# Hybrid Mamba-2 and latent-attention trunk on one core: probabilities of whole off-diagonal chunks split with queries on partitions and turned by DMA

## The chip, the cores and the metric

The kernel runs on one core of one Trainium2 chip. A core has a matrix engine (TensorE, PE in the profile), a vector engine (VectorE, DVE), a scalar engine (ScalarE, ACT), a general engine (GpSimd, POOL) and a queue engine that mostly issues transfers (SyncE, SP). They run side by side, each takes its instructions in order, and they wait for each other through semaphores. Sixteen DMA engines move data for all. The metric is the device time of one execution in microseconds; the median of several executions is given.

## The reference: what is computed

Two layers over 2048 tokens of width 1024: a Mamba-2 layer (in-projection, causal convolution, chunked state-space scan, gated out-projection), then a latent-attention layer with 16 heads whose keys and values come once from a compressed latent; a final RMS norm. The change lies in the attention:

```python
for i in range(S // Q_BLOCK):
    q0 = i * Q_BLOCK
    kv_len = q0 + Q_BLOCK
    s = einsum('bqhd,bkhd->bhqk', q_nope[:, q0:kv_len], k_nope[:, :kv_len]) + \
        einsum('bqhr,bkr->bhqk', q_rope[:, q0:kv_len], k_rope[:, :kv_len])
    s = s.astype(float32) * scale
    mask = (q0 + local)[:, None] >= arange(kv_len)[None, :]
    p = softmax(where(mask, s, -inf), axis=-1)
    outs.append(einsum('bhqk,bkhd->bqhd', p, v[:, :kv_len]))
```

A query sees the keys up to its own place, so the work of a block of queries grows with its place in the sequence. Queries and keys have 96 numbers a head (64 and 32 rotary), values 64.

## The kernel before, in words

The program has three stages: the Mamba layer with the projections of the attention (`layers`, L212), the attention itself (`attention`, L855, and `heads`, L863), and the gated output projection with the final norm (`back`, L999). Tiles are placed and semaphores set by a tile framework, which also chooses the order of each engine's instructions; in the attention PE's order alone is that of the program text (L860).

All products are made of parts: a float32 number is split into a high part and a remainder, and three products stand for one (`mm3`, L83). Score products use this; probabilities and values are split into two float16 halves (`pair16`, L114), with the value halves side by side, so that two products do.

`heads` goes over 64 jobs: 16 heads, and in each four blocks of 512 queries (`qb` 0 to 3). It has two streams. The first, `scores` (L879), takes the 128 queries of `j` = 0 to 3 in turn; I call this a row. Its keys, `512*qb + 128*(j+1)`, are cut by `cuts` (L868) into chunks of up to 512, one PSUM bank each: one bank for `qb` 0, up to four for `qb` 3. For each chunk PE makes three products (L85 to L87), a mask is added at the row's last chunk (L903, L905), and DVE takes the maximum over the keys (L906). After the last chunk DVE reduces the maxima to the bias (L910). The exponentials (L918, ACT) write the probabilities `Pr` to SBUF and their sums aside; they are kept in the list `late` and issued one by one with the score products that follow, and the row's sums are added by DVE (L922). The score banks have the tag "mm" with four buffers, so PE cannot start a chunk before the exponential of the chunk four before it has read its bank.

The second stream is the value products. A unit is a block of 128 keys for 512 queries. `turn` (L928) transposes the four 128 x 128 probability blocks on PE (L933) into a bank "tr", and `pair16` splits that bank: ACT writes the high half (L116), DVE the remainder (L117), both scaled by `PSCALE`. `values` (L939) multiplies both halves with the values (L943, L944) into a bank that collects the job's output; the last unit calls `finish` (L948), where ACT copies the bank (L950), SP stores one half (L952) and POOL adds the other in an accumulating store (L956).

PE alternates between the streams by a table written by hand: `CREDIT[qb][j][n]` (L43) says after each score chunk which turns ("T") and value products ("V") follow. They start 20 chunks late (`LAG`), and two turned units are held ahead (`DEPTH`). Loads of the next head's queries, keys and values are issued on POOL (L833 to L847), the output projection's weights on SP (L852). `back` splits those weights by ACT and POOL (L1016, L1017) into tiles "W", which have buffers of their own beside the attention's, and "K", which take over key buffers.

## Time and profile before

| | |
|---|---|
| median of 3 runs | 3239.51 us (3238.54 to 3240.34) |
| the profiled execution | 3238.15 us |
| its span, first to last instruction | 3236.3 us |
| mean granted clock of TensorE | 0.995 |
| busy: PE, DVE, ACT, POOL | 98%, 80%, 64%, 20% of the span |

How to read the rows: a row of the groups names line, engine, operation, tile written and read, shape and count, then the busy time of the group, the mean duration of one in ns, and the idle time before them with what ended it. A row of the waits says which engine and line waited for which, in total, how often and how long at most. Matmuls are pipelined: a row's duration is longer than the step from one start to the next, so PE's cost of one is read from starts in the timeline. The small operations of DVE overlap a little in the same way, so sums of durations come out above the busy time.

### The profile page before, as it was taken

Reading aid. Unit: us, or ns where it says so; the run is one execution under the profiler, and the core shown is the slowest. Engines: PE = TensorE matmul, PEld = TensorE weight load, DVE = VectorE, ACT = ScalarE, POOL = GpSimd, SP = SyncE. Lnnn points to the kernel's source line nnn. Section 1 sums busy time; section 2 is a strip of 40 time slices with the busy share of each in tenths; the row PEclk is TensorE's granted clock in tenths of the full one; section 3 lists DMA queues with packets and bytes.
Section 4 is the critical chain, followed back from the end, with each engine's and each line's share of the span. In section 5 each row is a group of like instructions: output and inputs, shape, how many; then the busy total and the mean of one; then the engine's idle time right before and its main releaser. Section 6 shows DMA issues by size and latency. Waiting matters only on the chain.

```text
span 3236.3 us, 50476 instructions
## 1 busy us (share of the span) xinstructions
PE 3156.2 (98%) x16708; PEld 2563.4 (79%) x16708; DVE 2593.4 (80%) x5490; ACT 2055.2 (64%) x5117; POOL 646.2 (20%) x842
## 2 busy tenths in 40 slices
PE   8999999999999999998999999999999999999998
PEld 6788888888888888887888888777777777777787
DVE  6988888889889888887776765668888888888675
ACT  5666666666657655666555554567777877778522
POOL 1221122221212222222211211222212212223100
PEclk9999999999999999999999999999999999999999
DMA  5333343333433334333466666753443434344385
GB/s 174 108 104 92 118 131 119 105 96 122 140 96 109 90 125 145 104 94 111 132 221 212 236 204 208 246 137 79 82 89 77 97 77 88 77 90 116 81 272 172
DMA packets 210572, 418.91 MB, mean 129 GB/s; under 512 B 27107, under 2 KB 68835, under 8 KB 208869
## 3 DMA queue, kind: packets, MB, share of 16 engines
q1 hardware_dynamic: 168900, 291.39, 28.9%
q0 software_dynamic: 41408, 124.29, 15.7%
q8 instruction: 132, 2.16, 0.3%
q14 instruction: 132, 1.07, 0.1%
HBM read 321.33 MB, written 94.24 MB: 128 GB/s over the span
## 4 chain that ended last, share of the span: by engine, by line
PE 44%; ACT 3%; DMA 2%; DVE 2%; issue 1%; SPq 0%; POOL 0%; ACTq 0%; DVEq 0%
PE mm L85 7%; PE mm L87 7%; PE mm L86 7%; PE tr L933 6%; PE tr L943 3%; PE tr L944 3%; PE tr L86 3%; PE tr L87 3%; PE tr L85 3%; ACT Pr L918 1%; DVE PTs L117 1%; ACT PTs L116 1%; DMA wraw<-in_kv_w_up_dram 1%; PE mm L905 1%; DMA wraw<-in_kv_w_down_dram 0%
## 5 line engine op out<-in xcount | busy, mean ns | idle before, releaser
L117 DVE SCALAR_TENSOR_TENSOR PTs<-tr,PTs 128x512 f16<-128x512 f32 (+3 forms) x640 | 374.7, 607 | 92.6 <-ACT PTs L116 86.0
L116 ACT ACTIVATE PTs<-tr 128x512 f16<-128x512 f32 (+3 forms) x640 | 328.2, 541 | 140.9 <-PE tr L933 140.0
L906 DVE TENSOR_REDUCE mx<-mm 128x1 f32<-128x512 f32 (+2 forms) x631 | 375.5, 607 | 45.4 <-PE mm L87 42.8
L918 ACT ACTIVATE Pr<-mm,nm 128x512 f32<-128x512 f32 (+2 forms) x631 | 395.1, 635 | 23.1 <-DVE nm L910 21.5
L108 ACT ACTIVATE wsp<-wraw 128x512 fp32r<-128x512 f32 (+1 forms) x452 | 251.1, 574 | 171.7 <-PE mm L87 82.4
L109 DVE TENSOR_TENSOR wsp<-wraw,wsp 128x512 fp32r<-128x512 f32 (+1 forms) x452 | 301.8, 680 | 69.7 <-ACT wsp L108 68.9
L85 PE MATMUL mm<-xT,wsp 128*128 128x512 f32 x800 | 321.0, 401 | 0.0
L933 PE MATMUL tr<-pack,Pr 128*128 128x128 f32 x2176 | 317.5, 273 | 0.9 <-ACT Os L950 0.8
L87 PE MATMUL mm<-xT,wsp 128*128 128x512 f32 x800 | 314.1, 393 | 0.0
L86 PE MATMUL mm<-xT,wsp 128*128 128x512 f32 x800 | 312.9, 391 | 0.0
L85 PE MATMUL mm<-K,xT 96*128 96x512 f32 (+2 forms) x639 | 286.7, 449 | 23.1 <-ACT Pr L918 21.7
L933 PEld LDWEIGHTS tr<-pack,Pr 128*128 128x128 f32 x2176 | 253.4, 141 | 49.3 <-ACT Os L950 1.6
L85 PE MATMUL mm<-wsp,xT 128*128 128x512 f32 (+1 forms) x640 | 242.1, 378 | 0.0
L86 PE MATMUL mm<-wsp,xT 128*128 128x512 f32 (+1 forms) x640 | 237.7, 371 | 0.0
L87 PE MATMUL mm<-wsp,xT 128*128 128x512 f32 (+1 forms) x640 | 237.5, 372 | 0.0
L87 PE MATMUL mm<-K,xT 96*128 96x512 f32 (+2 forms) x639 | 231.4, 362 | 0.0
L358 DVE SCALAR_TENSOR_TENSOR cacc<-craw,pack,cacc 128x512 f32<-128x512 f32 x288 | 216.5, 774 | 18.3 <-ACT cacc L356 17.8
L86 PE MATMUL mm<-K,xT 96*128 96x512 f32 (+2 forms) x639 | 231.1, 362 | 0.0
L496 POOL TENSOR_TENSOR Xp<-Xw,Xp 128x512 fp32r<-128x512 f32 x64 | 83.1, 1298 | 697.5 <-ACT Xp L495 393.1
L943 PE MATMUL tr<-PTs,xT 128*128 128x512 f16 (+3 forms) x640 | 222.0, 348 | 0.1
L538 ACT ACTIVATE Xw<-tr,d_wend 128x64 f32<-128x64 f32 x512 | 182.8, 358 | 58.7 <-DVE Xd L534 58.6
L944 PE MATMUL tr<-PTs,xT 128*128 128x512 f16 (+3 forms) x640 | 219.4, 347 | 0.0
(368 smaller groups left out, 8145.9 us busy)
## 6 DMA issues: line engine op xcount, KB each, us to landing
wraw<-in_ssm_w_in_dram SPq DMA_DIRECT2D x256, 256.0 KB, 2.8
big<-cumT SPq DMA_DIRECT2D x64, 512.0 KB, 4.0
wraw<-in_ssm_w_out_dram SPq DMA_DIRECT2D x128, 256.0 KB, 2.6
wraw<-in_ssm_w_in_dram SPq DMA_DIRECT2D x129, 128.0 KB, 2.2
xT<-qn_d POOLq DMA_DIRECT2D x64, 256.0 KB, 4.4
K<-kn_d POOLq DMA_DIRECT2D x15, 1024.0 KB, 9.2
wraw<-in_mla_w_uq_dram SPq DMA_DIRECT2D x36, 256.0 KB, 4.0
hx<-in_x_dram SPq DMA_DIRECT2D x16, 512.0 KB, 4.2
```

The costliest lines, as they stand in the source:

```text
L85: mm(out, l_hi, r_hi, start=start, stop=False)
L86: mm(out, l_hi, r_lo, start=False, stop=False)
L87: mm(out, l_lo, r_hi, start=False, stop=stop)
L108: nc.scalar.activation(hi, src, AF.Copy)
L109: nc.vector.tensor_tensor(lo, src, hi.bitcast(F32), ALU.subtract)
L116: self.nc.scalar.activation(hi, src, AF.Copy, scale=scale)
L117: self.nc.vector.scalar_tensor_tensor(lo, src, scale, hi, ALU.mult, ALU.subtract)
L906: v.tensor_reduce(mx[:, n:n + 1], s[:, :w], AX.X, ALU.max)
L918: nc.scalar.activation(x[:, :w], s[:, :w], AF.Exp, bias=nm, accum_out=sm[:, n:n + 1])
L933: nc.tensor.transpose(pt[:, j * P:(j + 1) * P], st["P"][j][kb], self.ident)
L943: nc.tensor.matmul(st["O"][:, c], vals[h][:, kb, :], u[:, 0], start=kb == 0, stop=False)
L944: nc.tensor.matmul(st["O"][:, c], vals[h][:, kb, :], u[:, 1], start=False, stop=kb == nk - 1)
```

## The change

Probabilities of chunks that lie wholly left of the diagonal block can be turned in another way. `BYDMA = (0, 1, 1, 2)` says for how many leading chunks of a row, by `qb`, this is done: none in `qb` 0, one in `qb` 1 and 2, two in `qb` 3. There, after the exponential, DVE casts the 128 x 512 probabilities to float16 with the queries still on the partitions, POOL subtracts to get the remainder, and SP issues a transposing DMA of the 128 x 1024 pair into a tile `PX`, from which the value products read directly. The scale moves into the exponential's bias (`PSHIFT`, the logarithm of 32768), since halves are now taken before the turn.

The bias is built up: maxima are taken negated, and from a row's second chunk on a small DVE operation keeps the running minimum with the shift added. `cuts` keeps a first chunk of 512 whole (a row of 640 keys is cut 512 + 256 rather than 384 + 256, the mask covering the surplus).

The table is replaced by a rule. Within a job DMA-turned and PE-turned units are mixed by `order`. A job's units may be issued only `GAP` = 5 chunks after its last score chunk. Each score chunk then allows an amount of turning and value work, in estimated microseconds (`T_US`, `V_US`), in proportion to its width; 85% of it is held back until the row's last chunk. The tiles "W" of the last stage move to a pool that is opened after the attention's is closed.

```diff
-CREDIT = (
...
-)
+GAP = 5
+BYDMA = (0, 1, 1, 2)
+T_US, V_US, S_US = 0.436, 0.432, 0.7
-PSCALE = 32768.0
+PSHIFT = 10.397207708399179
...
-    def pair16(self, hi, lo, src, scale=1.0):
-        self.nc.scalar.activation(hi, src, AF.Copy, scale=scale)
-        self.nc.vector.scalar_tensor_tensor(lo, src, scale, hi, ALU.mult, ALU.subtract)
+    def pair16(self, hi, lo, src):
+        self.nc.scalar.activation(hi, src, AF.Copy)
+        self.nc.vector.tensor_tensor(lo, src, hi, ALU.subtract)
...
-                if kv - at == TB + P:
+                if kv - at == TB + P and at:
...
-                    v.tensor_reduce(mx[:, n:n + 1], s[:, :w], AX.X, ALU.max)
+                    m = mx[:, n:n + 1]
+                    v.tensor_reduce(m, s[:, :w], AX.X, ALU.max, negate=True)
                     banks.append((s, w))
-                    yield CREDIT[qb][j][n]
-                nm = self.t(sp, "nm", [P, 1], bufs=4)
-                v.tensor_reduce(nm, mx[:, :nb], AX.X, ALU.max, negate=True)
+                    if n != 0 or nb == 1:
+                        nm, old = self.t(sp, "nm", [P, 1], bufs=6), nm
+                    if nb == 1:
+                        v.tensor_scalar(nm, m, PSHIFT, None, ALU.add)
+                    elif n == 1:
+                        v.scalar_tensor_tensor(nm, m, mx[:, 0:1], shift, ALU.min, ALU.add)
+                    elif n > 1:
+                        v.scalar_tensor_tensor(nm, m, shift, old, ALU.add, ALU.min)
+                    yield qb, w, n == nb - 1
...
                     nc.scalar.activation(x[:, :w], s[:, :w], AF.Exp, bias=nm, accum_out=sm[:, n:n + 1])
+                    if n < BYDMA[qb]:
+                        u = self.t(sp, "Ph", [P, 2, TB], F16, bufs=4)
+                        v.tensor_copy(u[:, 0], x)
+                        nc.gpsimd.tensor_tensor(u[:, 1], x, u[:, 0], ALU.subtract)
+                        if j == 0:
+                            st["X"].append(self.t(sp, "PX", [P, 2, 4, TB], F16, bufs=5))
+                        d = st["X"][n].rearrange("p s k q -> p (s k) q")[:, :, j * P:(j + 1) * P]
+                        nc.sync.dma_start_transpose(d, u.rearrange("p s k -> p (s k)"))
...
+        def order(qb):
+            d, p = list(range(4 * BYDMA[qb])), list(range(4 * BYDMA[qb], 4 * qb + 4))
+            return sorted(d + p, key=lambda kb: kb / len(d) if kb in d else (kb - len(d) + 0.5) / len(p))
...
+        def action(limit):
+            n, a = todo[0] if todo else (len(jobs), None)
+            ready = a and (by_dma(a) or a[:3] in turned)
+            if turns and turns[0][0] < limit and (len(turned) <= DEPTH or not ready):
+                b = turns.pop(0)[1]
+                turned[b[:3]] = turn(*b)
+                return T_US * (4 - max(b[2] - 4 * b[1], 0)) / 4
+            if not ready or n >= limit:
+                return 0
+            todo.pop(0)
+            h, qb, kb, st = a
+            if by_dma(a):
+                x = st["X"][kb // 4]
+                values(*a, (x[:, 0, kb % 4], x[:, 1, kb % 4]), slice(0, TB))
+            else:
+                values(*a, *turned.pop(a[:3]))
+            return V_US * (4 - max(kb - 4 * qb, 0)) / 4
...
+        for n, qb, w, last in ahead():
+            step += 1
+            ended[n] = step
+            limit = max([k + 1 for k in ended if k < n and ended[k] + GAP <= step], default=0)
+            if step <= LAG:
+                continue
+            share = 1.06 * rate * w
+            kept += share if last else share * 0.85
+            if last:
+                allowed, kept = allowed + kept, 0.0
+            else:
+                allowed += share * 0.15
+            while allowed > 0:
+                t = action(limit)
+                if not t:
+                    allowed = min(allowed, 2.0)
+                    break
+                allowed -= t
...
-                    W.append(self.t(self.wo, "W", [P, 2, 2, TB], F32R, bufs=4))
+                    W.append(self.t(sp, "W", [P, 2, 2, TB], F32R, bufs=4))
```

More of the change, by code (lines that the diff above doesn't have):

```diff
@@ L973, in ahead @@
                     sums[h] = self.t(sp, "sum", [P, 16], bufs=3)
-                yield from scores(h, qb, states[n])
-        units = [(h, qb, kb, states[n]) for n, (h, qb) in enumerate(jobs) for kb in range(4 * qb + 4)]
-        held = []
-        def work(what):
-            if what == "T" and units:
-                a = units.pop(0)
-                held.append((a, turn(*a)))
-            elif what == "V" and held and (len(held) > DEPTH or not units):
-                a, (u, c) = held.pop(0)
-                values(*a, u, c)
@@ L988, in heads @@
-        step = 0
-        for credit in ahead():
-            step += 1
-            if step > LAG:
-                for what in credit:
-                    work(what)
-        while units or held:
-            work("T")
-            work("V")
+                for step in scores(h, qb, states[n]):
+                    yield (n, *step)
+        def order(qb):
+            d, p = list(range(4 * BYDMA[qb])), list(range(4 * BYDMA[qb], 4 * qb + 4))
+            return sorted(d + p, key=lambda kb: kb / len(d) if kb in d else (kb - len(d) + 0.5) / len(p))
@@ new lines, in by_dma @@
+        def by_dma(unit):
+            return unit[2] // 4 < BYDMA[unit[1]]
+        todo = [(n, (h, qb, kb, states[n])) for n, (h, qb) in enumerate(jobs) for kb in order(qb)]
+        turns = [x for x in todo if not by_dma(x[1])]
+        turned = {}
+        def action(limit):
[15 more added lines that the diff above has]
+            return V_US * (4 - max(kb - 4 * qb, 0)) / 4
@@ L999, in back @@
+        while action(len(jobs)):
+            pass
     def back(self):
```

34 lines of the change are left out of this document (19 added, 15 removed).

## The prediction

> **What bounds the kernel now.** I read the page first, for the engines' shares and the granted clock.
>
> ```profile
> span 3236.3 us, 50476 instructions
> PE 3156.2 (98%) x16708; PEld 2563.4 (79%) x16708; DVE 2593.4 (80%) x5490; ACT 2055.2 (64%) x5117; POOL 646.2 (20%) x842
> PEclk9999999999999999999999999999999999999999
> ```
>
> TensorE (PE) is nearly always busy and its clock is not throttled. The diff touches the attention alone, so next come the windows that cut it out. Columns: window, its length, then busy time of PE, weight loads, VectorE (DVE), ScalarE (ACT), GpSimd (POOL), granted clock, DMA share, GB/s.
>
> ```profile
> 2128.00:2150.00 22.00, 20.85 (x116) 15.63 (x116) 19.00 (x57) 17.43 (x54) 9.68 (x17) 1.00 0.73 159
> 2150.00:3050.00 900.00, 877.11 (x5542) 671.30 (x5540) 752.89 (x1775) 714.95 (x1956) 191.67 (x278) 1.00 0.41 83
> ```
>
> Attention is 922 us; DVE is busy 772 of them (0.84), ACT 732, POOL 201. Third, the waits inside the long window (total, times, longest).
>
> ```profile
> POOL xT L845 <- PE tr L962: 187.2, 14, 13.6
> POOL o_d L956 <- DMA o_d<-Os: 151.7, 16, 23.7
> PEld mm L85 <- ACT Pr L918: 53.8, 112, 2.4
> PE mm L85 <- ACT Pr L918: 20.8, 19, 1.9
> ```
>
> PE's only large wait is the first score product waiting until an exponential (L918) has emptied a score bank: 75 us in the weight-load and matmul rows together. There are four such banks, and a row of 2048 keys takes all four, so the next row cannot start before maximum, bias and exponential of the last are through. What PE does meanwhile is turning (L933) and value products (L943, L944); I call these filler. So the stage is bound by PE's work plus the part of that chain that filler does not cover. Durations come from the profiled execution, 3238.15 us with a span of 3236.3; the median of the runs is 1.4 above it, which I add at the end.
>
> **The change part by part.** PE's price is its issue spacing, not the modelled duration; the timeline of PE shows it (start, duration).
>
> ```profile
> 2602.04 0.40 PE L85 MATMUL mm<-K,xT 96*128 96x512 f32 x1
> 2602.28 0.39 PE L86 MATMUL mm<-K,xT 96*128 96x512 f32 x1
> 2602.51 0.40 PE L87 MATMUL mm<-K,xT 96*128 96x512 f32 x1
> 2602.75 0.23 PE L905 MATMUL mm<-mk,idb 128*128 128x128 bf16 x1
> ...
> 3045.45 0.60 PE L933 MATMUL tr<-pack,Pr 128*128 128x128 f32 x4
> 3045.88 0.38 PE L943 MATMUL tr<-PTs,xT 128*128 128x512 f16 x1
> 3046.10 0.38 PE L944 MATMUL tr<-PTs,xT 128*128 128x512 f16 x1
> 3046.32 0.27 PE L933 MATMUL tr<-pack,Pr 128*128 128x128 f32 x1
> ```
>
> A score of 512 keys costs 0.71 us, a turn of four transposes 0.43, its two value products 0.44.
>
> Removed from PE: per head, four 128-key blocks each of query blocks 1 and 2 and eight of block 3 are now turned by DMA; times 16 heads, 256 turns. 256 x 0.43 = 110 us, all on the path. Their value products stay. Added to PE: rows of 640 keys are cut 512 + 256 instead of 384 + 256, 128 columns more in 16 rows: 16 x 0.71/4 = 3 us, and their wider masks about 1. Net -106.
>
> The prices on the other engines:
>
> ```profile
> L117 DVE SCALAR_TENSOR_TENSOR PTs<-tr,PTs 128x512 f16<-128x512 f32 x448 | 300.2, 687 | 77.1 <-ACT PTs L116 70.5
> L918 ACT ACTIVATE Pr<-mm,nm 128x512 f32<-128x512 f32 x395 | 270.7, 694 | 16.8 <-DVE nm L910 15.2
> L906 DVE TENSOR_REDUCE mx<-mm 128x1 f32<-128x512 f32 x395 | 269.0, 685 | 44.6 <-PE mm L87 42.8 <-PE mm L905 0.3
> L116 ACT ACTIVATE PTs<-tr 128x512 f16<-128x512 f32 x448 | 258.4, 600 | 89.1 <-PE tr L933 88.2
> L918 ACT ACTIVATION_READ_ACCUMULATOR Pr<-mm,nm 128x1 f32 x631 | 136.2, 216 | 0.0
> L154 DVE SCALAR_TENSOR_TENSOR rsy<-rsq,rsy 128x1 f32<-128x1 f32 x12 | 1.9, 160 | 0.4
> L645 DVE CAST sz<-yt 128x512 f32<-128x512 int32 x4 | 1.7, 421 | 0.6 <-DMA yt<-in_positions_dram 0.6
> L496 POOL TENSOR_TENSOR Xp<-Xw,Xp 128x512 fp32r<-128x512 f32 x64 | 83.1, 1298 | 697.5 <-ACT Xp L495 393.1 <-issue 194.2 <-PE tr L87 70.1
> L524 DVE TENSOR_SCALAR big<-big,d_cum 128x128 f32<-128x128 f32 x512 | 138.2, 315 | 18.0 <-DMA big<-cumT 18.0
> L456 DVE TENSOR_SCALAR big<-big 128x128 f32<-128x128 f32 x28 | 6.3, 225 | 0.1
> ```
>
> ACT loses 256 x 0.60 = 154 us: 578 busy, further from the bound than before. DVE loses 256 x 0.687 = 176; gains 256 casts to f16, for which I take L645's 0.42 (a converting copy of the same size, SBUF to SBUF): +108; and as the running minimum replaces one small reduction per row by one small operation per bank after the first, 192 more at 0.16: +31. So 772 - 37 = 735. The other forms (subtract instead of multiply-subtract, the scale moved into the bias) change no count; nothing for them. A cast could cost up to 0.42 + 1.30 if each had to wait out a GpSimd subtraction: this end is kept for a rival. POOL gains 256 subtractions at L496's 1.30, 333 us: 534 busy, but its queue is in order, and the rows above show its loads waiting up to 13.6 us and its accumulating store up to 23.7. In the order of the new program most subtractions stand ahead of the load or store that would hold them; the ones behind feed chunks first used 9 us of PE work or more later, so I count nothing.
>
> Filler lost. Counting the two programs' PE orders with the prices above, mean filler after the last score of a row goes from 2.20 to 1.63 us for rows of four banks, from 0.68 to 0 for one bank; for three banks filler inside and after goes from 2.12 to 1.87, with more of it (1.58 against 1.41) after the last score, where it counts; two-bank rows keep theirs (1.60 to 1.65, part now inside). Four banks: the chain after the last score is reduce 0.69, bias 0.16, exponential 0.69, at least 1.54, and DVE arrives late: its four reduces of 0.69 take as long as the four scores of 0.71, and small operations, casts and subtractions come on top. PE waits here already, so I take lost filler as wait: 64 rows x 0.57 = +36. Three banks gain 64 x 0.17 = -11. One bank: four such rows follow each other with nothing between, while ACT empties a bank in 0.69 + 0.22 at full width; PE needs 0.56 a row: about 0.35 x 64 = +22. Sum of waits +47; bounds: 0 (filler was in excess) and +95 (both prices doubled, DVE late as well).
>
> The DMA path. A transfer of 256 KB per transpose, 256 of them, is new on SP's queue; no row shows one. The nearest rows:
>
> ```profile
> q1 hardware_dynamic: 7568, 14.15, 5.5%
> o_d<-Os SPq DMA_DIRECT2D x64, 128.0 KB, 3.3
> xT<-o_d SPq DMA_DIRECT2D x2, 256.0 KB, 4.8
> wraw<-in_ssm_w_in_dram SPq DMA_DIRECT2D x256, 256.0 KB, 2.8
> ```
>
> SP's plain traffic used 5.5% of the DMA engines for 14.15 MB of the window; 67 MB at that price are 26%, beside the 0.41 there: no bound. Latency: 2.8 to 4.8. The tightest use is the first value product of block 3's first chunk: 5.4 us of PE work after the last score that feeds it, by the new order. The chain is 0.69 + 0.16 + 0.69 + 0.42 + 1.30 + 2.8 = 6.1, or 8.1 with 4.8, so 0.7 to 2.7 us too long. In the same stretch lie the four one-bank rows with their 1.4 us of wait per head, which counts for both. I take 0 and keep 16 x 1.3 = 21 as the bound. The store of the output waits on SP between transposes, but for a copy that is due before them. Other blocks have 9 us or more. New waits: a cast waits until the transpose four before it has read its buffer (uses four apart lie at least 5.5 us of PE work from each other), and behind it on DVE stand the next row's reduces; a subtraction waits for its cast, and behind it on POOL stand the loads of the next head's queries, keys and values, due most of a head later; a transpose waits for its subtraction, and behind it on SP stand the output stores, which only POOL's accumulating store waits for.
>
> The first weights of the last product now come from a pool freed only after attention. Two of eight are still made early, 24 x 0.23 = 5.5 us of PE work each, so the third has 11 us against one ACT copy and one POOL subtraction at twice L496's width, some 4: nothing.
>
> Sum: -106 + 47 = -59; 3238.15 - 59 + 1.4 = 3180. I predict 3179.
>
> **The rivals.** *Full gain*: the waits on exponentials stay as they are, for ACT and DVE are both relieved. 3238 - 106 = 3132, with 1.4, 3133. For it: ACT's 154 us less. Against: the filler that covered the chain is what was removed.
>
> *DVE held by GpSimd.* L524 takes 315 ns where L456 takes 225 at the same size, both within SBUF: something lengthens the former by 0.09. By that row casts cost 256 x 0.09 = 23 more, in a DVE that has spare time outside the four-bank rows. As a mechanism: in a four-bank row two casts come 0.91 apart (0.69 + 0.22); if the second must wait until GpSimd's subtraction of the first is done, it loses 0.42 + 1.30 - 0.91 = 0.8 in front of the next row's reduces; 64 rows, 52 us: 3231. The Trainium skill, "SBUF — State Buffer", section "Who interferes with whom", has this as its rule: a VectorE copy or cast in a two-port mode and a GpSimd instruction exclude each other, and the later one waits the whole instruction. By that rule the sum is 3231, by the rows 3179 to 3202; the trace shows the lengthening, not a whole block.
>
> *Transposes one at a time (slower)*. If SP's queue finishes one transpose before the next moves, 256 x t is a floor of the stage: it decides from 922/256 = 3.6 us. At 2.8 it does nothing; at 4.0 the stage is 1024 and the time 3341; at 4.8 1229 and 3546. For it: 16-bit pieces, turned, should cost more than plain rows of the same bytes, and 3.3 to 4.8 are the attention's own latencies. Against: those are latencies, which overlap. The Trainium skill, "DMA: Bandwidth & Descriptors", section "Latency and other measured facts", gives 261 GB/s for a transposing DMA; an estimate from it is 1.0 us for 256 KB, by which this rival would not come and the sum stays. No row here shows one.
>
> *No change*: DVE's share at 0.84 is already its limit; then 735/0.84 = 875 and 3238 - 47 = 3191, which is still faster, so no change needs two mishaps at once.
>
> **How the numbers follow.** Forecast 0.45 (3155 to 3205); full gain 0.20; DVE held 0.12; within 0.2% (6.5 us, about what a measurement here can tell) 0.04; transposes one at a time 0.19. Faster 0.45 + 0.20 + 0.11 = 0.76 (part of DVE held ends within 0.2%, which makes same 0.05), slower 0.19. The range leaves out full gain's best tail (below 3125, 0.05) and the slower rival from a transpose of 3.7 us up (above 3275, 0.13).
>
> **What would show it.** Transposes at L933's place down from 2176 to 1152, PE's spacing unchanged; the wait of the first score on the exponential, 75 now, at about 120; casts near 0.42 (0.8 more in pairs shows the exclusion); SP's transposes landing in 3 to 5 us with less than 3.6 between starts; value products on DMA-turned tiles waiting under 21 us in all. The prediction is wrong if that last wait is the longest of the stage, or if PE waits no longer than before.

## The result, and the profile after

The changed kernel is slower: 3402.24 us median (3385.28 to 3417.8) against 3239.03 us before; the ratio is 1.0504, 95% interval 1.045 to 1.0557. The profiled execution took 3407.87 us. The prediction (3179, range 3125 to 3275) is wrong in its sign.

The first lines of the page of the changed kernel: span, engines, granted clock.

```profile
span 3405.5 us, 49623 instructions
PE 3162.6 (93%) x15684; PEld 2500.2 (73%) x15684; DVE 2662.5 (78%) x5683; ACT 1948.8 (57%) x4861; POOL 942.7 (28%) x1098
PEclk9999999999999999999999999898898998989999
```

There are 1024 matmuls fewer, as the change says, and TensorE is busy 93% instead of 98%; from the start of the attention its clock is no longer full. The window over nearly the whole of the attention, columns as in the prediction:

```profile
2150.00:3215.00 1065.00, 890.47 (x4573) 614.60 (x4572) 816.83 (x1971) 609.67 (x1715) 470.76 (x527) 0.91 0.77 132
```

The stage has become 159 us longer (922 to 1081 us, table below). The records of the granted clock in it are either full or half, so 0.91 means that some 190 us ran at half rate. VectorE is busy not for less time but for more (817 us), in part because its operations take longer (below), and the DMA share has gone from 0.41 to 0.77. Next the waits of the same stretch (who waits for whom, total, times, longest):

```profile
...
PEld mm L84 <- ACT Pr L927: 163.3, 169, 6.3
...
POOL o_d L975 <- DMA o_d<-Os: 111.7, 26, 19.7
PE mm L84 <- ACT Pr L927: 96.1, 114, 4.6
...
PE tr L962 <- DMA PX<-Ph: 53.8, 13, 6.6
...
PEld L962 <- DMA PX<-Ph: 21.2, 5, 6.2
```

The first score product's wait for an exponential is now 259 us in the two rows where it was 75, and a wait that did not exist stands beside it: the value product that waits for a tile turned by DMA (PX), up to 6.6 us at a time.

To see where the time goes I took, from the timeline of PE, each start less the start before it less the price of the instruction before it (score of 512 columns 0.2325 us, transpose 0.109, value product 0.216, mask 0.067, in proportion to the columns). What is left over is waiting or half clock, and is put to what came next:

| kernel | attention | sum of prices | left over at scores | at turnings | at value products |
|---|---|---|---|---|---|
| before | 922.2 | 878.8 | 38.4 | 2.9 | 1.3 |
| changed | 1081.5 | 772.7 | 178.6 | 21.7 | 103.1 |

TensorE's work fell by 106 us, which is the prediction's -106. Everything else went wrong: +140 at the scores, +102 at the value products, +19 at the turnings. The groups of VectorE and GpSimd in the same window (busy, mean ns of one):

```profile
...
L116 DVE TENSOR_TENSOR PTl<-tr,PTh 128x512 f16<-128x512 f32 (+3 forms) x384 | 207.6, 552 | 97.7 <-ACT PTh L115 95.3
L931 DVE CAST Ph<-Pr 128x512 f16<-128x512 f32 x250 | 146.3, 587 | 92.8 <-ACT Pr L927 43.0 <-issue 42.4 <-DMA PX<-Ph 6.7
L916 DVE SCALAR_TENSOR_TENSOR nm<-mx,shift 128x1 f32<-128x1 f32 x185 | 83.5, 451 | 1.4
L918 DVE SCALAR_TENSOR_TENSOR nm<-mx,shift,nm 128x1 f32<-128x1 f32 x189 | 49.1, 260 | 1.7
```

```profile
L932 POOL TENSOR_TENSOR Ph<-Pr,Ph 128x512 f16<-128x512 f32 x250 | 302.4, 1238 | 347.3 <-DVE Ph L931 233.6 <-DVE sum L940 113.3
```

The subtraction costs what was predicted (1.24 us for 1.30). But a bias operation on one number per partition takes 260 to 451 ns in the mean, and its spread over the whole execution (min/median/max) shows that a few take thousands (nine of these 192 take over 1 us):

```profile
L916 DVE SCALAR_TENSOR_TENSOR nm<-mx,shift x192: 203/217/5337, 2135.4 to 3196.4; 128x1 f32<-128x1 f32 x192
```

Last, one change of heads, by the timelines of GpSimd, of SP's queue and of PE (start, duration; in brackets the idle time before and what ended it):

```profile
2708.27 0.87 POOL L975 DMA_DIRECT2D o_d<-Os  x1 [6.48 <-ACT Pr L927]
2708.86 1.47 POOL L932 TENSOR_TENSOR Ph<-Pr,Ph 128x512 f16<-128x512 f32 x1
2709.98 0.85 POOL L844 DMA_DIRECT2D xT<-qn_d  x1
2710.60 0.74 POOL L845 DMA_DIRECT2D xT<-q_d  x1
2711.13 2.48 POOL L932 TENSOR_TENSOR Ph<-Pr,Ph 128x512 f16<-128x512 f32 x2
```

```profile
2710.36 1.24 SPq L936 DMA_TRANSPOSE PX<-Ph  x1
2711.69 0.54 SPq L971 DMA_DIRECT2D o_d<-Os  x1
2712.53 3.09 SPq L936 DMA_TRANSPOSE PX<-Ph  x2
```

```profile
2710.25 0.23 PE L906 MATMUL mm<-mk,idb 128*128 128x128 bf16 x1
2716.03 0.61 PE L962 MATMUL tr<-PX,xT 128*128 128x512 f16 x1 [5.55 <-DMA PX<-Ph]
2716.43 0.63 PE L963 MATMUL tr<-PX,xT 128*128 128x512 f16 x1
```

GpSimd stood 6.48 us at an accumulating output store, with the subtraction of block 3's chunk behind it, and two loads ahead of the next two subtractions. So the chunk is turned late, TensorE stands 5.55 us, and then takes 0.61 to 0.63 us for a value product instead of 0.38. This happens about once a head.

### The profile page after: what moved, and what is told of

It is laid out like the page before. It is cut to its first block, busy times and chain, and to the rows that moved or that the text cites. A ratio compares the mean times of both kernels' runs of the same rounds, so it can differ in the third digit from the quotient of the medians.

```text
span 3405.5 us, 49623 instructions
## 1 busy us (share of the span) xinstructions
PE 3162.6 (93%) x15684; PEld 2500.2 (73%) x15684; DVE 2662.5 (78%) x5683; ACT 1948.8 (57%) x4861; POOL 942.7 (28%) x1098
## 5 line engine op out<-in xcount | busy, mean ns | idle before, releaser
L908 DVE TENSOR_REDUCE mx<-mm 128x1 f32<-128x512 f32 (+2 forms) x631 | 376.1, 609 | 47.5 <-PE mm L86 19.8
L932 POOL TENSOR_TENSOR Ph<-Pr,Ph 128x512 f16<-128x512 f32 x256 | 309.4, 1237 | 350.9 <-DVE Ph L931 237.2
L84 PE MATMUL mm<-K,xT 96*128 96x512 f32 (+2 forms) x639 | 306.7, 480 | 100.7 <-ACT Pr L927 100.0
L115 ACT ACTIVATE PTh<-tr 128x512 f16<-128x512 f32 (+3 forms) x384 | 182.6, 491 | 312.0 <-PE tr L951 310.2
L116 DVE TENSOR_TENSOR PTl<-tr,PTh 128x512 f16<-128x512 f32 (+3 forms) x384 | 207.6, 552 | 97.7 <-ACT PTh L115 95.3
L84 PEld LDWEIGHTS mm<-K,xT 96*128 96x128 f32 x639 | 128.1, 200 | 201.7 <-ACT Pr L927 168.2
L86 PE MATMUL mm<-K,xT 96*128 96x512 f32 (+2 forms) x639 | 245.1, 383 | 0.0
L85 PE MATMUL mm<-K,xT 96*128 96x512 f32 (+2 forms) x639 | 244.4, 383 | 0.0
L931 DVE CAST Ph<-Pr 128x512 f16<-128x512 f32 x256 | 149.5, 585 | 93.0 <-ACT Pr L927 43.0
L84 PE MATMUL mm<-wsp,yT 128*128 128x512 f32 x512 | 206.6, 407 | 3.3 <-ACT wsp L110 3.3
```

The lines of the kernel that those rows point to most:

```text
L84: mm(out, l_hi, r_hi, start=start, stop=False)
L85: mm(out, l_hi, r_lo, start=False, stop=False)
L86: mm(out, l_lo, r_hi, start=False, stop=stop)
L115: self.nc.scalar.activation(hi, src, AF.Copy)
L116: self.nc.vector.tensor_tensor(lo, src, hi, ALU.subtract)
L908: v.tensor_reduce(m, s[:, :w], AX.X, ALU.max, negate=True)
```

## The experiments

Four candidates were to be told apart: the chunk that comes late; VectorE locked, that is, held up, by GpSimd's subtraction; the running bias; and the time-paced order. A run's edit is shown against the kernel that it starts from, with its main lines alone; `...` stands for lines left out. All times are medians; the kernel before measured 3240 to 3243 us beside them.

**The late chunk: e1_late.** The value products of DMA-turned units go to the end of their block.

```diff
-            return sorted(d + p, key=lambda kb: kb / len(d) if kb in d else (kb - len(d) + 0.5) / len(p))
+            return p + d
```

> The DMA-turned chunks' value products go to the end of their block instead of being spread between the others; nothing else is changed, and the score rows get the same amounts of filler. By the kernel's own order the tightest use then stands 15.4 us of PE work behind the last score of its chunk instead of 5.4 us. Theory 'late chunk' (PE stands at the value products of block 3 for a chunk that the DMA has not yet turned, then runs at half the granted clock for some 10 us): the waits for PX (75 us by the groups of waits of the changed kernel) go, with one of the two clock drops per head: 3280 to 3320 us. Theory 'locked vector engine' (the bias operations and casts of VectorE stretch beside GpSimd's subtraction, so that the exps and with them the first score products are late): the first-score waits stay as they are: 3370 us or more. Theory 'no filler' (the paced order leaves one-bank rows bare): 3370 us or more too.

Measured: 3345.29 us, ratio 1.0317 (1.0298 to 1.0336), 57 us faster than the changed kernel. No wait of PE for PX is left among its waits, and half-clock time (by the granted clock of its windows) falls from some 190 to 120 us. The late chunk is shown as a cause, of about a third of the loss; its expected 80 to 120 us were too many.

**The bias in two operations: e2_bias, and both: e4_bias_late.** The bias is made once a row.

```diff
...
-                    elif n == 1:
-                        v.scalar_tensor_tensor(nm, m, mx[:, 0:1], shift, ALU.min, ALU.add)
-                    elif n > 1:
-                        v.scalar_tensor_tensor(nm, m, shift, old, ALU.add, ALU.min)
+                    if n == nb - 1:
...
+                            v.tensor_reduce(old, mx[:, :nb], AX.X, ALU.min)
+                        v.tensor_scalar(nm, old[:, 0:1], PSHIFT, None, ALU.add)
```

> The bias of the exp is made at the end of each row by one reduction over the row's maxima and one addition of the constant; no operation with two SBUF inputs is left in the chain from the last score to the exp. Theory 'locked vector engine': the bias operations return from 260 to 450 ns to about 150 ns each and are no longer stretched to 2 us, the first-score waits (PE and its weight loads on Pr: 96 and 163 us) fall by about half, 3340 to 3350 us; the waits for PX stay. Theories 'late chunk' and 'no filler': 3390 us or more, unchanged within 0.4%.

> The edits of the first two together. If late chunks and the locked vector engine are both at work, their gains add: 3240 to 3270 us. If one alone is the cause, it equals that one's run within 0.5%. If neither ('no filler'), 3370 us or more.

Measured: e2 3380.14 us (1.0433, 1.0406 to 1.046), e4 3325.95 us (1.0252, 1.0236 to 1.0267). The new operations take 149 and 150 ns and are not lengthened, yet only 22 us come back, not 52 to 62, and that is hardly clear of the spread: the intervals of e2 (up to 1.046) and of the changed kernel (from 1.045) overlap. On top of the late chunk the same edit is worth 19 us, clear of noise, and the two together 76, about their sum. Both expectations held in their direction and were too large.

**No DMA turning at all: e3_nodma.**

```diff
-BYDMA = (0, 1, 1, 2)
+BYDMA = (0, 0, 0, 0)
```

> No chunk is turned by DMA (all turned by the TensorE as before the change); the new bias, the time-paced order and the 16 rows cut 512+256 stay. Mean filler after a score row by the order: 0 us in one-bank rows, 1.4 in two-bank, 2.2 in three-bank, 2.7 in four-bank rows. Theory 'no filler': slower than the kernel before by itself, 3270 to 3300 us, with first-score waits in the first blocks. Theories 'late chunk' and 'locked vector engine': the loss goes altogether with the casts, the subtraction and the transposing DMAs, 3235 to 3250 us.

Measured: 3319.01 us (1.0234, 1.0219 to 1.025). This was the surprise: without one cast, subtraction or transposing DMA the rest of the change loses 76 us. The next runs take it apart.

**The order, the bias and the cut: e5_lists, e9_lists_bias, e13_lists_one, e14_pace_one.** e5 is e3 with the hand-written lists of the kernel before:

```diff
-                    yield qb, w, n == nb - 1
+                    yield CREDIT[qb][j][n]
...
+            if step > LAG:
+                for what in credit:
+                    work(what)
```

> As the run without DMA turning, but the order of turnings and value products is again the one written out by hand in the kernel before; the new bias and the 16 rows cut 512+256 stay. Theory 'order' (the time-paced order by itself costs the 76 us that the run without DMA lost): 3235 to 3255 us. Theory 'bias or cuts' (two-input bias operations or the new cut cost it): 3290 us or more.

e9 is e5 with the bias of e2, a reduction and an addition:

> As the run with the hand-written lists and no DMA turning, but with the one-reduction bias in place of the running one; the 16 rows cut 512+256 stay. Theory 'bias on the path' (384 two-input bias operations at 211 ns and 64 additions against 256 reductions at 151 ns are some 51 us of VectorE, where the four-bank rows have no slack): at 256 reductions or additions more than the kernel before the loss falls from 50 to 10 to 25 us, 3250 to 3266 us. Theory 'cuts': it stays within 8 us of 3291 us.

Measured: e5 3291.24 us (1.0161, 1.0146 to 1.0176), e9 3291.2 us (1.0155, 1.014 to 1.0171). The same loss with both biases seemed to leave the cut. The timelines of e5 say otherwise. VectorE, then ScalarE, then PE behind the third row of block 3 (j = 2, four banks):

```profile
2466.68 0.54 DVE L914 TENSOR_REDUCE mx<-mm 128x1 f32<-128x384 f32 x1
2467.15 0.21 DVE L924 SCALAR_TENSOR_TENSOR nm<-mx,shift,nm 128x1 f32<-128x1 f32 x1
2467.52 0.69 DVE L122 TENSOR_TENSOR PTl<-tr,PTh 128x512 f16<-128x512 f32 x1 [0.17 <-ACT PTh L121]
2468.13 0.21 DVE L924 SCALAR_TENSOR_TENSOR nm<-mx,shift,nm 128x1 f32<-128x1 f32 x1
```

```profile
2467.70 1.08 ACT L121 ACTIVATE PTh<-tr 128x512 f16<-128x512 f32 x2 [0.21 <-PE tr L957]
2468.67 0.69 ACT L933 ACTIVATE Pr<-mm,nm 128x512 f32<-128x512 f32 x1
```

```profile
2466.12 0.23 PE L912 MATMUL mm<-mk,idb 128*128 128x128 bf16 x1
...
2469.50 0.51 PE L90 MATMUL mm<-K,xT 96*128 96x512 f32 x1 [0.97 <-ACT Pr L933]
```

Between the last two bias operations of the row, which depend on one another, the scheduler has put the remainder of a turned unit (L122, 0.69 us), which itself waits for ScalarE. The bias comes 0.98 us after the operation that it depends on, ScalarE has meanwhile begun two high halves (L121), and the exponential starts 2.55 us after the mask; TensorE stands 0.97 us. The time from a row's mask to its first exponential, mean over 13 heads, and what was left over at the scores of the row after it (all 16 heads):

| after row (query block, j) | before | e5 | e9 | e13 |
|---|---|---|---|---|
| block 2, j=0 | 2.12 us, 0.1 us | 2.13, 1.2 | 3.04, 14.5 | 2.12, 1.4 |
| block 2, j=3 | 1.32, 0.3 | 2.25, 14.8 | 2.19, 13.7 | 1.33, 0.6 |
| block 3, j=2 | 1.26, 1.4 | 2.55, 19.8 | 2.55, 19.8 | 1.26, 1.5 |
| block 3, j=3 | 1.29, 0.4 | 2.20, 13.6 | 1.39, 1.3 | 1.29, 0.4 |

In these rows the wait comes and goes with the chain. If that is the cause, a bias of one operation, which nothing can split, must bring all of it back. e13 is e5 with the single negated reduction of the kernel before, and the factor 32768 again in the split of turned units; the 16 rows cut 512 + 256 stay:

```diff
...
+                    if n == nb - 1:
+                        nm = self.t(sp, "nm", [P, 1], bufs=6)
+                        v.tensor_reduce(nm, mx[:, :nb], AX.X, ALU.max, negate=True)
```

> As the run with the hand-written lists and no DMA turning, but the bias is again the one negated reduction of the kernel before, and the factor 32768 is again in the split of the turned unit; the 16 rows cut 512+256 stay. Theory 'split chain' (the scheduler puts a remainder between two dependent bias operations; one operation can't be split): 3240 to 3252 us. Theory 'cut' (the 16 rows of 512+256): 3285 us or more.

Measured: 3247.23 us (1.0021, 1.0011 to 1.003). 44 us come back; the cut is not the cause, and with what else differs it costs 7 us, 3.4 of them TensorE work. e14 gives the same bias to the time-paced order of e3:

> The run without DMA turning (time-paced order, 3319 us) with the one-operation bias and the factor of the kernel before. Theory 'split chain' alone: the 50 us go, 3265 to 3280 us, and what remains over 3245 us is the paced order's own (its waits at the value products were 45 us). Otherwise: 3300 us or more.

Measured: 3309.37 us (1.0213, 1.0198 to 1.0229). So the theory "split chain" missed here: the paced order alone costs 62 us, and the split chain costs only 10 there (e3 less e14) where it cost 44 in the lists. The waits of TensorE and its weight loads in e14 say where:

```profile
PE tr L955 <- ACT PTh L115: 11.4, 28, 1.4
PE tr L955 <- ACT Os L962: 10.3, 15, 1.0
PE mm L84 <- ACT Pr L920: 7.8, 34, 0.7
PE tr L956 <- DVE PTl L116: 6.7, 16, 1.9
```

```profile
PEld mm L84 <- ACT Pr L920: 39.4, 96, 1.2
PEld L956 <- issue: 30.9, 47, 1.5
```

The first score waits no more than before (37 us left over in all, 36 in e13). The value products do (L955 and L956): 55 us are left over against 0.9. Sorted by unit, about 23 us of it stand at the last units of blocks 1 and 2. There this order has used up the held units, because the next block may not be turned yet, so turning and value product follow one another and TensorE waits for the two halves. Another 23 us stand at the first units of blocks 0 and 3, where two more units are held: there the product waits for ScalarE's copy of an output (`Os` above) or for a remainder on VectorE. Why these come late was not tried.

**GpSimd's subtraction: e7_no_subtract, e10_act_cast, e12_no_gpsimd.** e7 is e4 without the subtraction; the low half that the DMA turns is a constant zero, so the remainder of these probabilities is missing:

```diff
-                        u = self.t(sp, "Ph", [P, 2, TB], F16, bufs=4)
-                        nc.gpsimd.tensor_tensor(u[:, 1], x, u[:, 0], ALU.subtract)
+                        u = halves[0]
```

> On top of the one-reduction bias and the DMA-turned products put last: GpSimd's subtraction is left out and the low half that the DMA turns is a constant zero, so the remainder of the DMA-turned probabilities is missing from the result; casts, transposing DMAs and products are as many as before. Theory 'locked vector engine': casts and score maxima are no longer stretched, the chain from score to exp shortens: 3270 to 3305 us. Otherwise, with the waits set by the order alone: within 10 us of the parent's 3326 us.

Measured: 3269.04 us (1.0093, 1.0078 to 1.0109), 57 us faster than e4. Casts are back at 429 ns in the mean. e10 is e4 with the casts moved to ScalarE; the subtraction stays on GpSimd. In e12 the casts are ScalarE's too, and VectorE subtracts in GpSimd's place. The edit of e10:

```diff
-                        v.tensor_copy(u[:, 0], x)
+                        nc.scalar.activation(u[:, 0], x, AF.Copy)
```

> On top of the one-reduction bias and the DMA-turned products put last: ScalarE makes the casts of the DMA-turned chunks (256 at about 0.6 us, into its idle time of some 320 us) in place of VectorE (0.43 us free, up to 3.6 us beside the subtraction); GpSimd's subtraction stays. Theory 'locked vector engine': no VectorE operation of any length has SBUF inputs now, nothing is left to be stretched, 3265 to 3300 us (parent 3326, without the subtraction 3269). If the subtraction hurts in another way (late chunks, its own queue), 3315 us or more.

> On top of the casts by ScalarE: VectorE makes the subtraction too (256 at about 0.6 us, 150 us more on VectorE against the 110 us of casts taken off), GpSimd is out of it. Theory 'locked vector engine': within 15 us of the run with casts by ScalarE and subtraction by GpSimd, either way, since nothing locks in either; theory 'GpSimd's queue is late' (the chunk waits for its 1.3 us subtractions behind stores and loads): 15 to 40 us faster than that run; theory 'VectorE is the bound': 15 us or more slower than it.

Measured: e10 3324.5 us (1.0261, 1.0239 to 1.0283), no gain over e4; e12 3388.59 us (1.0451, 1.0433 to 1.0469). In e10 ScalarE has 728 us of work in place of 610, and its exponentials queue behind casts, so the run does not tell whether the lock or the loaded queue is at fault: inconclusive. e12, 64 us slower than e10, says that VectorE has no room for the subtraction.

**The spread of the filler and the banks: e6_even, e11_act_cast_order, e8_fifth_bank, e15_dma_one, e16_dma_one_order.** e6 is e4 with

```diff
-LAG = 20
+LAG = 28
...
-            share = 1.06 * rate * w
+            share = 1.0 * rate * w
```

> On top of the one-reduction bias and the DMA-turned products put last: the factor of the paced share 1.0 instead of 1.06 and the lag 28 score steps instead of 20. By the order itself the filler after the last score of a row goes from 0, 0.89, 1.70, 1.58 us in rows of one, two, three and four banks to 0.45, 1.03, 1.51, 2.10 us (kernel before: 0.68, 1.60, 1.41, 2.20). Theory 'order': the stalls at the first score product of a row (103 us of stalls over 0.7 us in the parent) fall by about half, and half-clock time with them: 3255 to 3290 us. If the filler is not what lacks: within 10 us of the parent's 3326 us.

Measured: 3352.45 us (1.0342, 1.0322 to 1.0361): slower by 27 us although the filler after the last score of a row comes nearer to that of the kernel before (by the expectation 0.45, 1.03, 1.51 and 2.10 us in rows of one to four banks, against 0.68, 1.60, 1.41 and 2.20). The amount of filler alone is not what decides; what made it slower was not found. e8 is e4 with

```diff
-"tr" if len(begun) <= 18 and len(begun) % 2 == 1 else "mm"
+"tr" if (len(begun) <= 18 and len(begun) % 2 == 1) or (len(begun) > 18 and qb == NB - 1 and n == 0) else "mm"
```

> On top of the one-reduction bias and the DMA-turned products put last: the first score of each four-bank row takes a PSUM bank of the other set, so five banks serve the scores there and the next row's first score need not wait for the first exp of this one. Theory 'round trip' (the first-score stalls are the wait for one bank's way from score over maximum and bias to exp): the first-score waits in four-bank rows fall to a fraction, 3250 to 3290 us. If they come from elsewhere, or turnings now lack banks: 3315 us or more.

Measured: 3328.24 us (1.028, 1.0261 to 1.0298), no change: the waits at the scores move from the first row of a head (23 us left over to 0.1) to its second (3 to 57). e11 is e10 with

```diff
-            kept += share if last else share * 0.85
+            kept += share if last else share
...
-                allowed += share * 0.15
+                pass
...
-                    allowed = min(allowed, 2.0)
+                    allowed = min(allowed, 0.4)
```

> On top of the casts by ScalarE: no filler is let go between the scores of a row (it all follows the row's last score), and at most 0.4 us instead of 2 us of it is saved up when nothing is ready. In the trace without the subtraction three turnings in a row fell into the second row of block 3, their three remainders on VectorE (1.89 us) went ahead of three score maxima, and the next row's first score stood 1.9 us. Theory 'bursts': the first-score stalls of that kind (36 us in that row, 20 us each in two others) go: 15 to 45 us faster than the run with the casts by ScalarE alone. If bursts matter not: within 8 us of it.

Measured: 3315.84 us (1.0228, 1.0213 to 1.0244), 9 us faster than e10: hardly more than no difference, and less than expected. e15 is e1 with the one-operation bias and no shift:

> The changed kernel with the DMA-turned products put last (3345 us) and with the bias as one negated reduction; the shift by 2^15 is left out, so the remainders of small probabilities lose bits. Theory 'split chain': 3275 to 3300 us, below both the parent and the two-operation bias (3326 us). If the DMA version's stalls come from missing filler and late exps for other reasons: 3315 to 3330 us.

Measured: 3297.2 us (1.0181, 1.0164 to 1.0198), 48 us faster than e1. e16 adds to it the two edits of e11 and a value product as the first piece after a row wherever two are turned:

> On top of the run before it: all filler follows the row's last score, at most 0.4 us is saved up, and the first piece after a row's last score is a value product wherever two are turned, so no turning's remainder gets ahead of the row's maximum on VectorE. If order decides the stalls: 15 to 45 us faster than the run before it. If not: within 10 us.

Measured: 3301.89 us (1.0182, 1.016 to 1.0204), the same. Moving pieces about within the paced order gives nothing here.

**DMA turning in the hand-written order: e17_lists_dma, and without the subtraction: e18_lists_dma_nosub.** This is e13 with the change's main part; a unit turned by DMA leaves its "T" in the list empty and comes last in its block. The factor 32768 is left out, as in e15.

```diff
-                held.append((a, turn(*a)))
+                held.append((a, None if by_dma(a) else turn(*a)))
```

> DMA turning of the same chunks in the hand-written order of the kernel before (a list's turning of a DMA-turned unit is simply empty; DMA-turned units last in their block) with one negated reduction as bias and no factor 2^15, so the remainders of small probabilities lose bits. Theory 'order' (the paced order's 62 us go here as well): about 3235 us, 3220 to 3250. Theory 'filler' (the 108 us of TensorE work that DMA turning saves were the cover of the chain from score to exp, so it comes back as waits and half clock whatever the order): 3255 us or more. A full gain (chain covered all the same) would be 3247 less 108: 3140 us.

> The run before it with GpSimd's subtraction left out, the DMA-turned low half a constant zero (the remainder of the DMA-turned probabilities is missing from the result). Theory 'locked vector engine': 30 to 60 us faster than the run before it, casts back at 0.43 us. If the subtraction's 57 us were only its part in the split chain: within 15 us of it.

Measured: e17 3285.66 us (1.0144, 1.0126 to 1.0161), e18 3184.71 us (0.9827, 0.9812 to 0.9842). By its number e17 falls to the theory "filler", but e18 shows that the subtraction is 101 us of it, more than its own theory gave it. One way in which it costs, the timelines of e17 show at a row of block 2, where the next head's keys and values are loaded: VectorE, GpSimd, PE.

```profile
2435.99 1.16 DVE L912 TENSOR_REDUCE mx<-mm 128x1 f32<-128x512 f32 x2 [0.39 <-PE mm L92]
2437.07 3.27 DVE L930 CAST Ph<-Pr 128x512 f16<-128x512 f32 x1
2440.26 0.14 DVE L939 TENSOR_REDUCE sum<-sm 128x1 f32<-128x2 f32 x1
2440.32 0.41 DVE L912 TENSOR_REDUCE mx<-mm 128x1 f32<-128x256 f32 x1
2440.76 0.16 DVE L917 TENSOR_REDUCE nm<-mx 128x1 f32<-128x3 f32 x1
```

```profile
2435.24 0.85 POOL L974 DMA_DIRECT2D o_d<-Os  x1 [10.85 <-ACT PTh L121]
2435.82 1.46 POOL L931 TENSOR_TENSOR Ph<-Pr,Ph 128x512 f16<-128x512 f32 x1
2436.93 0.82 POOL L839 DMA_DIRECT2D K<-kr_d  x1
2437.48 2.56 POOL L931 TENSOR_TENSOR Ph<-Pr,Ph 128x512 f16<-128x512 f32 x2
```

```profile
2438.70 0.38 PE L962 MATMUL tr<-PX,xT 128*128 128x512 f16 x1
2441.85 0.50 PE L90 MATMUL mm<-K,xT 96*128 96x512 f32 x1 [2.77 <-ACT Pr L926]
...
2443.28 0.63 PE L961 MATMUL tr<-PX,xT 128*128 128x512 f16 x1
```

GpSimd waits 10.85 us at the output store; three subtractions have piled up behind it and then run nearly without a gap. A cast of 0.43 us that starts meanwhile takes 3.27, until the last of them is done. Behind it on VectorE stand the row's last maximum and its bias, and TensorE stands 2.77 us and soon runs at half rate (0.63 us for 0.38). In front of the rows j = 0 to 2 of block 2, e17 leaves over 76 us at the scores, e18 17.

That is not all of the 101 us. In e17 casts also stand for another reason: the halves `Ph` have four buffers, and a cast waits until a transposing DMA has read the one that it is to write. First the sum of these waits in e17, then the longest, on VectorE, GpSimd and PE:

```profile
DVE Ph L930 <- DMA PX<-Ph: 59.1, 16, 13.2
...
2509.85 0.43 DVE L930 CAST Ph<-Pr 128x512 f16<-128x512 f32 x1 [13.17 <-DMA PX<-Ph]
...
2510.48 0.86 POOL L974 DMA_DIRECT2D o_d<-Os  x1 [26.59 <-DMA o_d<-Os]
...
2511.79 0.79 PE L90 MATMUL mm<-K,xT 96*128 96x512 f32 x1 [13.18 <-ACT Pr L926]
```

The three longest stalls of TensorE in e17 (13.2, 5.6 and 5.1 us) are of this kind. In the longest, GpSimd stood at its store for a transfer of SP's in the same time, so the transfers themselves were late; why is not shown. Sorted by what VectorE did in the 2.5 us before them, 43 us of the stalls over 0.5 us follow a cast that stood for a buffer, 29 us a cast that was held, 15 us both and 48 us neither; in e18 it is 10, 2, 0 and 43 us. The rest of the 101 us is mostly half clock (75 us of the attention at half rate in e17, 17 in e18). So the subtraction's 101 us are the held VectorE and the late buffers together, and no run parts the two. In the changed kernel casts stood only once for a buffer (6.7 us). The window over the attention of e18, its casts, and the bias reductions of e17, where GpSimd subtracts (min/median/max):

```profile
2150.00:2992.00 842.00, 794.07 (x4561) 565.35 (x4562) 693.18 (x1787) 595.16 (x1715) 183.43 (x275) 0.99 1.07 167
```

```profile
L934 DVE CAST Ph<-Pr x256: 408/419/1582, 2139.7 to 2980.5; 128x512 f16<-128x512 f32 x128
...
L917 DVE TENSOR_REDUCE nm<-mx x256: 94/147/158, 2133.2 to 3071.5; 128x1 f32<-128x1 f32 x32, 128x1 f32<-128x2 f32 x32, 128x1 f32<-128x3 f32 x32, 128x1 f32<-128x4 f32 x32
```

In e18 the clock is nearly full again (0.99), the casts take 0.42 us in the median and stand for a buffer three times (10 us in all), at a DMA share of 1.07.

The decomposition of the main runs, in us, as in the table above (the window of all of them begins with the first score):

| kernel | time | attention | prices | scores | turnings | value products |
|---|---|---|---|---|---|---|
| e13 lists, one-operation bias | 3247 | 924.4 | 882.2 | 36.1 | 4.2 | 0.9 |
| e14 paced, one-operation bias | 3309 | 984.6 | 883.5 | 37.0 | 8.2 | 55.0 |
| e3 paced, running bias | 3319 | 993.6 | 883.5 | 64.2 | 8.0 | 36.9 |
| e1 changed, DMA units last | 3345 | 1020.7 | 771.4 | 161.1 | 12.5 | 71.4 |
| e15 the same, one-operation bias | 3297 | 962.2 | 771.4 | 118.5 | 10.0 | 59.3 |
| e17 lists, DMA, one-operation bias | 3286 | 953.4 | 769.3 | 148.7 | 22.2 | 11.6 |
| e18 the same, no subtraction | 3185 | 859.2 | 769.3 | 80.8 | 2.1 | 6.2 |

No run with the whole computation is faster than the kernel before. e18 is, but lacks the remainder. Whether e17 gains when the accumulating store leaves GpSimd's queue, with more buffers for the halves, or with a remainder made elsewhere, was not tried.

## Why the prediction was wrong

**TensorE's work, -106: right.** The sum of prices fell by 106.1 us.

**Filler lost, +47: the total came out, by luck.** Between e13 and e18, the hand-written lists without and with turning by DMA, prices fall by 113 us and the scores' leftover rises by 45; the net is -62, where the prediction had -59. But the prediction had counted the paced order, and its terms do not match: left over after rows of four banks are 30 us more (predicted +36), after rows of three banks 10 more (-11), after rows of one bank 1 more (+22), after rows of two 4 more (0). And e18 leaves the remainder out. What holds is that turning by DMA without the subtraction gains about 60 us, because lost filler takes back part of TensorE's saving. The wrong part is what was set at nothing.

**"POOL gains 256 subtractions ... so I count nothing": wrong, the largest step.** The subtraction is worth 101 us in the hand-written order, 57 in the paced one. The rows that the prediction quoted pointed at it: an accumulating store that waits up to 23.7 us. With subtractions behind it, they come late and in a bunch. The rival "DVE held by GpSimd" had the mechanism, with 0.12 and 52 us: it let a cast wait for one subtraction in four-bank rows only, and the trace shows a cast held through a bunch, in rows of three banks. The prediction also named the cast's wait for a buffer and priced it at nothing, since uses four apart lie at least 5.5 us of work apart; in e17 it came to 59 us. The Trainium skill, "SBUF — State Buffer", section "Who interferes with whom", states that a VectorE cast in a two-port mode, or an operation with two SBUF inputs, excludes a reading GpSimd instruction, and that reductions never contend. The traces agree: beside GpSimd's subtractions the bias with two SBUF inputs took up to 5.34 us (L916 above), e17's cast 3.27, and none of the reductions that make the bias in e17 over 0.158. They also show one VectorE instruction held for longer than a single GpSimd instruction, 1.24 us, lasts; the prediction had weighed one.

**"192 more bias operations at 0.16: +31" in a VectorE total that falls: wrong.** The operation takes 0.21 us where nothing holds it, but it is not the total that counts. The prediction counted how many, and not where they stand: a chain of two dependent operations lets the scheduler place a remainder between them. This is worth 44 us in the lists (e5 less e13) and 48 with DMA turning (e1 less e15), in which the lock has a share; in the paced order without DMA it is 10.

**The paced order priced by its filler alone: wrong.** Of its 62 us (e14 less e13), 54 are waits at value products that the kernel before did not have (1.3 us left over there): some 23 us where no other turned unit is held, and as many at the first units of two blocks. No term of the sum stood for them. The "0.35 x 64 = +22" for one-bank rows without filler was about twice too large: rows 1 to 3 of the heads leave over 20 us in the changed kernel, but 11 in e15, where the late chunk and the split chain are gone. The term had set ScalarE's price at full width, 0.91 us, against TensorE's mean over these rows, which are 256 to 512 keys wide.

**"I take 0 and keep 21" for the first chunk of block 3: wrong.** The prediction had found the place and the 0.7 to 2.7 us that the chain is too long, but not what GpSimd's queue adds to it. The waits for PX are 75 us in the two groups (53.8 for the products and 21.2 for their weight loads), about 4 us a time, and putting those products last gives 57 us back. Of the signs of error that the prediction named, the wait for PX became TensorE's longest single wait with a cause named (6.6 us against 6.3 for the first score), though not the largest in total.

**The clock was not thought of.** Long stalls of TensorE are followed by instructions at half rate (0.61 to 0.63 us for 0.38 above), so a long wait costs more than itself; the stalls of about 1 us in e5 brought 3.4 us at half rate in all. Some 190 us at half rate are up to 95 us lost in the changed kernel; in e18, at 0.99 over 842 us, up to 8.

**The rival "transposes one at a time": did not come.** The 256 transposing DMAs hold SP's queue for 1.24 us each in the median and land in a median of 4.0 us, above the 3.6 from which that rival was to decide if one had to finish before the next moves. It did not: the stage of e18, with as many of them, takes 859 us, where 256 x 4.0 would be 1024.

The losses add up only as a chain of runs: 7 us for the cut and the rest, 62 for the order, 10 for the running bias in it, and 83 for turning by DMA on top (changed less e3) make the 163. In that 83 are 110 us of saved work against lost filler, the late chunk, the locked VectorE and the clock, which these runs do not part further.

## What to carry to other kernels

A price of zero for work on an idle engine holds only if nothing blocks that engine's queue, and if nobody waits for it within the longest wait in that queue: look there first. In a chain that ends a wait, count dependent instructions and what a scheduler may put between them, not their total time. When a change does three things, run each alone: here turning by DMA gained 62 us in the old order once the subtraction was left out, under losses that hid it.

## What was not expected of the hardware

A VectorE operation on a single number per partition took up to 5.34 us beside GpSimd's subtractions (median 0.217), and casts up to 3.6 us in e17 (median 0.427). In e17 TensorE stood 2.77 us, and the granted clock was at half 1 us later, while the kernel before, with stalls of up to 1.9 us, kept a granted clock of 1.00 over its attention. The clock's records in e17 are at half for 3.41 us or a multiple of it. If its attention is cut into stretches of 3.41 us on the same grid, every one at full clock in which TensorE idled for 1.96 us or more is followed by half clock, and none in which it idled for 1.79 us or less; in the changed kernel the border is less sharp, between 1.2 and 1.6 us. A share of 1.07 of the DMA engines' time, by the profile's count, went with the fastest run of all, e18.
